# Ninety-two expert columns listed instead of 88, and three dense columns held back for the end of each PEER stage, in a two-layer decoder trunk on one core

## The chip, the core and the metric

The kernel runs on one core of a Trainium2 chip. A core has a matrix engine (PE), a vector engine (DVE), a scalar engine (ACT), GpSimd (POOL), a queue engine (SP) and 16 DMA engines. The metric is the device time of one execution in microseconds (us), as a median of several runs.

## The reference, cut to what matters

Two layers, 256 tokens of 1024 numbers, float32. Each layer is a token mixer, a layer norm, a PEER mixture of 16384 experts, a second layer norm and a gated addition:

```python
for i in range(DEPTH):                        # DEPTH = 2
    x = layer_norm(alpha * x + mix, ...)      # mix: SSD in layer 0, attention in layer 1
    ffn = peer_ffn(x, peer_w_q[i], peer_sub_keys[i], peer_u[i], peer_v[i])
    x = layer_norm(alpha * x + ffn, ln_ffn_g[i], ln_ffn_b[i])
    gate = jax.nn.sigmoid((x @ ple_w_gate[i]).astype(jnp.float32)).astype(x.dtype)
    x = x + gate * (p[i] @ ple_w_proj[i])

def block(xb):                                # in peer_ffn, 128 tokens at a time
    q = (xb @ w_q).reshape(PEER_TOKEN_BLOCK, PEER_HEADS, 2, PEER_HALF)
    ...                                       # 16 of 16384 experts for each token and head
    u_g = u[expert]
    v_g = v[expert]
    act = jax.nn.gelu(jnp.einsum('td,thkd->thk', xb, u_g).astype(f32))
    return jnp.einsum('thk,thkd->td', (gate * act).astype(v_g.dtype), v_g)
```

## The kernel before, in words

The experts of a layer are 128 columns of 128 experts. For every column the kernel computes the activations of all 256 tokens (`expert_in`, 16 matmuls against `u`) and multiplies them by the gates, which are zero for a token that did not pick the expert. Then the rows of `v` have to be summed with these weights. The 256 tokens are two blocks of 128; the sum lives in four PSUM banks, `accs[tb][h]`, block `tb` by half `h` of the 1024 outputs.

There are two ways to add a column. A **dense** column (`dense`, `expert_out`) loads 512 KB of `v` by the SP queue into a `raw` buffer, splits it on ACT (the high part, line 125) and DVE (the low part, line 126) into one of four `hl` buffers, splits its weights in the same way, and takes 12 matmuls of 512 columns: three products of high and low parts for each of the four banks (`mm3s`, line 151). The first `MANY` = 88 columns are **listed** instead. Their 88 x 128 experts are sorted into three classes by who picked them: both blocks, block 0 alone, block 1 alone; experts that nobody picked drop out. The picked ones are packed into groups of 128 (`CAPS`: 36 groups of `both`, 21 of `one`, 21 of `two`). A group fetches its 128 rows of `v`, and the 128 rows of weights that go with them, by two gathers on the POOL queue (line 1187), splits them like a dense column, and takes 12 matmuls if both blocks need it and 6 if one does. If a class has more experts than its groups hold, a loop behind a branch (`general`, `branch`) does all listed columns again for the surplus.

So that groups can fetch weights, the activations of the listed columns are written to DRAM (`keep`, 8 columns a call, ACT queue): block 0 twice, to a table for all groups (`w_d`) and to one for the `one` groups (`a_d`), and block 1 to `w_d`. The lists are made on DVE and PE in stages (`listing`, `stages`) that are laid under the last 12 `expert_in` steps and the first `LEAD` = 6 dense columns. `late(e)` finishes the activations of the last columns: it needs the sum of two halves that a POOL DMA `w<-w` (line 931) adds up in place, and then runs a GELU on ACT (line 950).

The order of the work is written out by hand. After the six leading dense columns come the 21 `one` groups mixed with `MIX` = 13 dense columns; then, in the part called **inner** here, the 36 `both` groups, 16 of the 21 `two` groups and the other 21 dense columns, spread evenly, with the loads of the gate weights (`w_pg`) among them; then the **tail**: the last `TAIL` = 5 `two` groups, which touch block 1 only. The last `both` group closes block 0, and the layer norm of block 0 (lines 205 to 226) runs on DVE, ACT and POOL while PE works on the five tail groups. The two transposes of the normed block (`turn`, line 191) stand on PE behind the fourth and the fifth of them (`TURNS`). Then come the gate matmuls (line 155).

An engine executes its instructions in the order in which they stand. Buffers come from pools: four `hl`, four `raw` of the SP queue, six `raw` and eight `rows_w` for gathers, five `w`.

Of the kernel before, what the change touches and what calls it, by code (L numbers as in the profile page):

```python
# [17 lines left out]
P = 128  # L18
T = 256
# [6 lines left out]
TAIL = 5  # L26
# [3 lines left out]
MANY = 88  # L30
# [5 lines left out]
CAPS = (36, 21, 21)  # L36
BASES = (0, 36, 57)
# [30 lines left out]
class Net:  # L68
# [688 lines left out]
    def peer(self, i):  # L757
        nc, dram = self.nc, self.dram
        with self.tc.tile_pool(name=f"peer{i}", bufs=1) as pool, ExitStack() as stack:
# [271 lines left out]
            def listing():  # L1031
# [73 lines left out]
                def place(j):  # L1105
                    if j == 0:
                        picked["list"] = self.aux()[:, :3 * MANY].rearrange("p (e k) -> p e k", k=3)
                    cs = slice(8 * j, 8 * j + 8)
                    o = ones[j % 2]
                    V.tensor_tensor(pairs(o), self.iota.rearrange("p (n j) -> p n j", j=2)[:, None].to_broadcast([P, 8, P // 2, 2]),  # L1110
                                    at_r[:, cs, None, :].to_broadcast([P, 8, P // 2, 2]), op=OP.is_equal)
                    for c in range(8):
                        nc.tensor.matmul(picked["list"][:, 8 * j + c], o[:, c], vals[:, 8 * j + c], start=True, stop=True)
# [36 lines left out]
                def ordered(k):  # L1150
                    with self.after((picked["turn"],) if k != 1 else ()):
# [4 lines left out]
                        *[lambda j=j: place(j) for j in range(MANY // 8)], keys, *[lambda k=k: ordered(k) for k in range(3)]]  # L1156
# [3 lines left out]
            def weights(e):  # L1160
                w = tl([P, 2, T], F32R, "w", 5)
                self.split(w[:, 0, :], w[:, 1, :], column(e))
                return w
# [4 lines left out]
            def expert_out(w, hl, start):  # L1168
                self.mm3s([(accs[tb][h], lambda a, tb=tb: w[:, a, tb * P:(tb + 1) * P],
                            lambda b, h=h: hl[:, b, h * 512:(h + 1) * 512]) for tb in range(2) for h in range(2)],  # L1170
                          start, lambda n: False)

            def fetched(s, hl=None):
                n = picked["n"] = picked["n"] + 1
                kind = sum(s >= b for b in BASES[1:])
                t = P if kind else T
                if kind == 1:
                    raw = early[n % 3][:, :1024] if n % 3 < 2 else self.raw()
                    some = early[n // 4 % 2][:, 1024 + P * (n % 4):1024 + P * (n % 4) + P]
# [11 lines left out]
                return kind, t, some, raw, hl  # L1191

            def group_load(s, hl=None):
                kind, t, some, raw, hl = fetched(s, hl)
                w = tl([P, 2, T], F32R, "w", 5)
                with self.after(picked["split"]):
                    self.split(w[:, 0, :t], w[:, 1, :t], some)
                    picked["split"] = self.split(hl[:, 0], hl[:, 1], raw)
                return kind, w, hl

            def group_out(kind, w, hl, ends=()):
                tbs = ((0, 1), (0,), (1,))[kind]
                self.mm3s([(accs[tb][h], lambda a, n=n: w[:, a, n * P:n * P + P],
                            lambda b, h=h: hl[:, b, h * 512:(h + 1) * 512]) for n, tb in enumerate(tbs) for h in range(2)],
                          False, lambda n: tbs[n // 2] in ends)

            def group(s):
                group_out(*group_load(s), (0,) if s == closing else ())

            def general():  # L1210
                raw, part, some = x[:, 0], pp[:, 0, :T], pp[:, 0, T:2 * T]
                hl, w = wide[0][:, 0], wide[0][:, 1, 0, :2 * T].rearrange("p (a t) -> p a t", a=2)
                with self.tc.For_i(0, MANY, 1) as c:
# [5 lines left out]
                    group_out(0, w, hl)  # L1219
# [8 lines left out]
            for hc in range(19):  # L1228
# [6 lines left out]
                if hc >= 7:  # L1235
# [13 lines left out]
            todo = [lambda c=c: keep(c, c + 8, 1) for c in range(0, MANY, 8)]  # L1249
# [38 lines left out]
            closing = [s for _, _, s in inner if s in both][-1]  # L1288
# [8 lines left out]
            wide = [new([P, 3, 2, 1024], "wide", F32R)]  # L1297
            pgw = {}

            def gate_load(n):  # L1300
                if n == 3:
                    wide.append(tl([P, 5, 2, 1024], F32R, "high"))
                hl = wide[0][:, n] if n < 3 else wide[1][:, n - 3]
# [15 lines left out]
            for k, (kind, w, hl) in enumerate(end):  # L1319
                group_out(kind, w, hl, (1,) if k == TAIL - 1 else ())  # L1320
# [135 lines left out]
```

## Time and profile before

| | |
|---|---|
| median of 3 runs | 1842.74 us (1841.68 to 1846.28) |
| the profiled execution | 1855.82 us, span 1854.0 us |
| PE busy | 1824.7 us, 98% of the span |
| weight loads of PE | 1554.5 us, 84% |
| DVE, ACT, POOL busy | 81%, 62%, 33% |
| mean DMA rate | 238 GB/s |
| mean granted PE clock | 0.995 of full speed |

The profiled execution is a single one and 13.1 us above the median. Times in the rows are microseconds from the start of its span. A busy PE is not a PE at its peak, since the ends of matmuls are modelled; how many matmuls finish in a stretch says more.

### The profile page before, as it was taken

The numbers are of one execution on the slowest core, as the hardware profiler recorded it, in microseconds if no ns is written. First come the engines' busy times: TensorE is split into PE (matmuls) and PEld (weight loads), VectorE is DVE, ScalarE is ACT, GpSimd is POOL, SyncE is SP. The second block draws the span as 40 slices with busy tenths as digits, with TensorE's granted clock in tenths as the row PEclk, the third lists the DMA queues.
The fourth block names the chain that finished last, engine by engine and source line by source line (L and its number), as shares of the span: only waits on it lengthen the run. The fifth ranks groups of instructions, "written<-read, shape, count | busy, mean of one in ns | idle before, by whom it ended". The sixth has DMA issues, their size and how long they took to land. (4 is left out here: it accounts for less than half of the span.)

```text
span 1854.0 us, 31864 instructions
## 1 busy us (share of the span) xinstructions
PE 1824.7 (98%) x11192; PEld 1554.5 (84%) x11192; DVE 1499.4 (81%) x2958; ACT 1157.6 (62%) x2322; POOL 604.0 (33%) x596
## 2 busy tenths in 40 slices
PE   8999999999999999999999999999999999989998
PEld 7998888888888888788877788888888887868887
DVE  7798789989989987676767778997998997657675
ACT  6865456697666656565646655669666665556563
POOL 0001003332222257766700001332222224776660
PEclk9999999999999999999999999999999999989999
DMA  7665669898799998989736566989779999888871
GB/s 263 204 192 177 218 181 228 218 238 203 183 273 331 270 314 277 333 271 321 268 100 199 182 205 189 225 218 244 195 185 283 320 282 284 284 291 283 313 241 55
DMA packets 211787, 442.13 MB, mean 238 GB/s; under 512 B 18756, under 2 KB 120296, under 8 KB 209960
## 3 DMA queue, kind: packets, MB, share of 16 engines
q1 hardware_dynamic: 77512, 275.14, 45.8%
q0 software_dynamic: 65472, 130.32, 27.3%
q10 hardware_dynamic: 68640, 34.61, 6.5%
q8 instruction: 89, 1.46, 0.3%
q14 instruction: 74, 0.61, 0.1%
HBM read 365.51 MB, written 40.93 MB: 219 GB/s over the span
## 5 line engine op out<-in xcount | busy, mean ns | idle before, releaser
L126 DVE TENSOR_TENSOR hl<-raw,hl 128x1024 fp32r<-128x1024 f32 x578 | 706.8, 1225 | 207.4 <-ACT hl L125 148.7
L167 PE MATMUL acc<-xT,hl 128*128 128x256 f32 (+1 forms) x4608 | 839.3, 339 | 2.0 <-DVE xT L194 0.8
L167 PEld LDWEIGHTS acc<-xT,hl 128*128 128x128 f32 x4608 | 700.7, 188 | 102.5 <-DVE hl L126 4.7
L125 ACT CAST hl<-raw 128x1024 fp32r<-128x1024 f32 x578 | 606.3, 1052 | 226.6 <-PE acc L151 108.4
L151 PE MATMUL acc<-hl,w 128*128 128x512 f32 x2316 | 538.4, 393 | 11.2 <-issue 3.6
L151 PEld LDWEIGHTS acc<-hl,w 128*128 128x128 f32 x2316 | 437.1, 190 | 110.5 <-issue 7.7
L931 POOL DMA_DIRECT2D w<-w x160 | 139.7, 873 | 392.9 <-ACT w L950 242.0
L931 POOL DMA_DIRECT2D act<-w x96 | 84.0, 875 | 303.8 <-ACT w L930 182.6
L1187 POOL DMA_INDIRECT raw<-in_v,r x128 | 141.3, 1104 | 94.8 <-DVE hl L126 35.4
L929 ACT COPY w<-acc 128x256 f32<-128x256 f32 x160 | 59.8, 374 | 165.3 <-PE acc L167 157.4
L1187 POOL DMA_INDIRECT rows_w<-w_d,r x114 | 132.1, 1159 | 34.7 <-issue 34.7
L155 PE MATMUL mm<-xT,hl 128*128 128x256 f32 x816 | 101.1, 284 | 2.1 <-ACT hl L125 1.0
L155 PEld LDWEIGHTS mm<-xT,hl 128*128 128x128 f32 x816 | 98.6, 192 | 3.7 <-ACT hl L125 1.5
L930 ACT COPY w<-acc 128x256 f32<-128x256 f32 x256 | 97.2, 380 | 0.0
L975 DVE TENSOR_TENSOR pick<-pick,r 128x2048 f16<-128x2048 f16 x64 | 78.2, 1222 | 0.9
L929 ACT COPY act<-acc 128x256 f32<-128x256 f32 x96 | 35.7, 372 | 69.1 <-PE acc L167 68.7
L991 PEld LDWEIGHTS <-pick 128*128 128x128 f16 x1024 | 66.4, 98 | 13.2 <-issue 11.1
L992 PE MATMUL mm<-pick 128*128 128x88 f16 x512 | 67.8, 203 | 0.0
L220 POOL TENSOR_TENSOR ln_s<-ln_s,mhalf 128x1 f32<-128x1 f32 x8 | 4.4, 552 | 179.2 <-PE acc L155 131.1
L542 POOL TENSOR_TENSOR sq<-sq,sqt 128x256 f32<-128x256 f32 x12 | 12.5, 1040 | 150.7 <-ACT sqt L541 150.4
L991 PE MATMUL aux<-pick 128*128 128x128 f16 x688 | 59.1, 220 | 0.5
L950 ACT ACTIVATE w<-w 128x256 f32<-128x256 f32 (+19 forms) x144 | 50.8, 353 | 8.7 <-DMA w<-w 8.7
(290 smaller groups left out, 2101.8 us busy)
## 6 DMA issues: line engine op xcount, KB each, us to landing
raw<-in_u SPq DMA_DIRECT2D x256, 512.0 KB
raw<-in_v SPq DMA_DIRECT2D x80, 512.0 KB
w_d<-act ACTq DMA_DIRECT2D x44, 512.0 KB
w<-w POOLq DMA_DIRECT2D x160, 128.0 KB
raw<-in_w_q SPq DMA_DIRECT2D x32, 512.0 KB
raw<-in_w_xbc SPq DMA_DIRECT2D x24, 512.0 KB
act<-w POOLq DMA_DIRECT2D x96, 128.0 KB
a_d<-act ACTq DMA_DIRECT2D x22, 512.0 KB
```

The costliest lines, as they stand in the source:

```text
L125: a = self.nc.scalar.copy(hi, src)
L126: b = self.nc.vector.tensor_tensor(lo, src, hi.bitcast(F32), op=OP.subtract)
L151: self.last_mm = self.nc.tensor.matmul(out, lhs(a), rhs(b), start=start and i == 0, stop=stop(n) and i == 2).ins
L155: self.last_mm = self.nc.tensor.matmul(out, lhs(a), rhs(b), start=start and i == 0, stop=stop and i == 2).ins
L167: self.nc.tensor.matmul(dst, hl[:, a, k * P:(k + 1) * P], src, start=k + a == 0, stop=(k, a) == order[-1] and k == KD - 1)
L929: nc.scalar.copy(whole, pe[:, :T])
L930: copied = nc.scalar.copy(pair[:, 1, :], pe[:, T:]).ins
L931: nc.gpsimd.dma_start(whole, pair[:, 1, :], accum_op=OP.add)
L975: nc.vector.tensor_tensor(a2, both, gates, op=OP.mult)
L991: nc.tensor.matmul(pg[:, t, :], one[:, 0, 4 * h + t], a2[:, 4 * h + t, k], start=k == 0, stop=k == 1)
L992: nc.tensor.matmul(banks["used"][:, MANY * tb:MANY * tb + MANY], one[:, 0, 4 * h + t], a2[:, 4 * h + t, 0, :MANY], start=at == 0, stop=at ...
L1187: got = nc.gpsimd.indirect_dma_start(out=dst, out_offset=None, in_=src, in_offset=rows(which))
```

## The change

The listed columns go from 88 to 92, and the groups from 36, 21 and 21 to 37, 22 and 22. The dense columns go from 40 to 36, and the last three of these (`LATER`) are not done in the inner part: their weights are split half-way through it, their `v` is loaded at its end, and their matmuls are cut in two. The halves for block 0 come first and close block 0. The halves for block 1 come behind, and then two `two` groups (`TAIL` = 2). The buffer `half` and a part of the tile `high` hold the high and low parts of the second of these groups, for which none of the four `hl` buffers is left. The list of 92 columns has one more step, of four columns.

```diff
-TAIL = 5
+TAIL = 2
+LATER = 3
-MANY = 88
+MANY = 92
-CAPS = (36, 21, 21)
-BASES = (0, 36, 57)
+CAPS = (37, 22, 22)
+BASES = (0, 37, 59)
...
             def keep_first():
-                c = kept[0]
-                if c + 8 <= min(now["ready"], MANY):
-                    keep(c, c + 8, 0)
-                    keep(c, c + 8, 0, first)
-                    kept[0] = c + 8
+                c, d = kept[0], min(kept[0] + 8, MANY)
+                if c < d <= now["ready"]:
+                    keep(c, d, 0)
+                    keep(c, d, 0, first)
+                    kept[0] = d
...
-            def expert_out(w, hl, start):
+            def expert_out(w, hl, start, tbs=(0, 1), ends=()):
                 self.mm3s([(accs[tb][h], lambda a, tb=tb: w[:, a, tb * P:(tb + 1) * P],
-                            lambda b, h=h: hl[:, b, h * 512:(h + 1) * 512]) for tb in range(2) for h in range(2)],
-                          start, lambda n: False)
+                            lambda b, h=h: hl[:, b, h * 512:(h + 1) * 512]) for tb in tbs for h in range(2)],
+                          start, lambda n: tbs[n // 2] in ends)
...
-            stages = [[classes], [*sums, ranks], [], [places, ones[0]], ones[1:3], ones[3:5], ones[5:7], ones[7:9], [*ones[9:11], surplus],
-                      [keys, one], [], [two], [both]]
+            stages = [[classes], [*sums, ranks], [], [places, ones[0]], ones[1:3], ones[3:5], ones[5:7], ones[7:9], ones[9:11],
+                      [ones[11], surplus], [keys, one], [], [two], [both]]
...
-            emit(inner, spread_over(dense, range(MANY + LEAD + MIX, P), 0.86), [(at, extra, f) for at, f in loads],
+            later = tl([P, LATER, 2, T], F32R, "pick", 2)
+            loads += [(0.5, lambda: [weights(P - LATER + k, later[:, k]) for k in range(LATER)])]
+            emit(inner, spread_over(dense, range(MANY + LEAD + MIX, P - LATER), 0.9), [(at, extra, f) for at, f in loads],
                  [(0.1, branch, None)])
-            end = []
-            for k, s in enumerate(last):
-                end.append(group_load(s, None if k else wide[1][:, 4]))
+            halves = [(later[:, k], self.chunk(dram["v"][i, P - LATER + k])) for k in range(LATER)]
+            end = [group_load(s, (half, wide[1][:, 8]) if k else None) for k, s in enumerate(last)]
+            for k, (w, hl) in enumerate(halves):
+                expert_out(w, hl, False, (0,), (0,) if k == LATER - 1 else ())
...
-            for k, (kind, w, hl) in enumerate(end):
-                group_out(kind, w, hl, (1,) if k == TAIL - 1 else ())
+            for k in range(LATER + TAIL):
+                if k < LATER:
+                    expert_out(*halves[k], False, (1,))
+                else:
+                    group_out(*end[k - LATER], (1,) if k == LATER + TAIL - 1 else ())
                 if k in TURNS[:2]:
                     self.turn(x, 0, TURNS.index(k))
```

Before, DVE at the end of layer 1: the splits of the last three tail groups (each a `w` and an `hl`) stand among the instructions of the norm of block 0, which begin with line 205.

```order
L126 TENSOR_TENSOR hl_19386<-raw_17921,hl_19386 128x1024
L126 TENSOR_TENSOR w_19395<-rows_w_17924,w_19395 128x128
L126 TENSOR_TENSOR hl_19394<-raw_17922,hl_19394 128x1024
L205 SCALAR_TENSOR_TENSOR last_17925,ln_s_19409<-last_17925,acc_17211 128x512
L126 TENSOR_TENSOR w_19403<-rows_w_17924,w_19403 128x128
L205 SCALAR_TENSOR_TENSOR last_17925,ln_s_19409<-last_17925,acc_17212 128x512
L126 TENSOR_TENSOR hl_19402<-raw_17923,hl_19402 128x1024
L207 TENSOR_SCALAR ln_s_19409<-ln_s_19409 128x1
L208 TENSOR_SCALAR ln_s_19409<-ln_s_19409 128x1
L218 SCALAR_TENSOR_TENSOR last_17928<-last_17925,ln_s_19409,last_17927 128x512 x2
```

The same place in the changed kernel, whose lines are numbered one higher here:

```order
L127 TENSOR_TENSOR hl_19311<-raw_19310,hl_19311 128x1024
L127 TENSOR_TENSOR hl_19316<-raw_19315,hl_19316 128x1024
L127 TENSOR_TENSOR hl_19321<-raw_19320,hl_19321 128x1024
L127 TENSOR_TENSOR hl_19327<-raw_17916,hl_19327 128x1024
L127 TENSOR_TENSOR w_19335<-rows_w_17921,w_19335 128x128
L127 TENSOR_TENSOR high_19151<-raw_17917,half_17927 128x1024
L206 SCALAR_TENSOR_TENSOR last_17922,ln_s_19359<-last_17922,acc_17183 128x512
L206 SCALAR_TENSOR_TENSOR last_17922,ln_s_19359<-last_17922,acc_17184 128x512
L208 TENSOR_SCALAR ln_s_19359<-ln_s_19359 128x1
L209 TENSOR_SCALAR ln_s_19359<-ln_s_19359 128x1
L219 SCALAR_TENSOR_TENSOR last_17925<-last_17922,ln_s_19359,last_17924 128x512 x2
```

The three dense splits (`raw_19310` to `raw_19320` come by the SP queue) and the two gathered ones (`raw_17916`, `raw_17917`) all stand ahead of the norm now, and nothing stands within it.

PE at that place in the changed kernel (`acc_17183` and `acc_17184` are block 0, `acc_17185` and `acc_17186` block 1, `pick_17928` the weights split early): the last matmuls of block 0, by the third held-back column, and the first of block 1, by the first.

```order
L152 MATMUL acc_17184<-hl_19321,pick_17928 128x512
L152 MATMUL acc_17183<-hl_19321,pick_17928 128x512
L152 MATMUL acc_17184<-hl_19321,pick_17928 128x512
L152 MATMUL acc_17185<-hl_19311,pick_17928 128x512
L152 MATMUL acc_17186<-hl_19311,pick_17928 128x512
```

Behind the close of block 0 stand 18 + 6 matmuls, then the first transpose, 6 matmuls and the second transpose; before, it was 24, the transpose, 6 and the transpose.

POOL where the lists are ready in layer 0, before: `w_7869`, `w_7910` and `w_7947` are the last three columns' sums, `pick<-a_d` and `pick<-in_v` the gathers of the first `one` groups (weights, then rows of `v`).

```order
L931 DMA w_7869<-w_7869 128x256
L1187 DMA pick_8104<-a_d_75,r_902_7452 128x128
L1187 DMA pick_8104<-in_v,r_902_7452 128x1024
L931 DMA w_7910<-w_7910 128x256
L1187 DMA pick_8104<-a_d_75,r_902_7452 128x128
L931 DMA w_7947<-w_7947 128x256
L1187 DMA pick_8105<-in_v,r_902_7452 128x1024
```

And in the changed kernel:

```order
L932 DMA w_7863<-w_7863 128x256
L932 DMA w_7904<-w_7904 128x256
L1189 DMA pick_8111<-a_d_75,r_902_7454 128x128
L1189 DMA pick_8111<-in_v,r_902_7454 128x1024
L932 DMA w_7954<-w_7954 128x256
L1189 DMA pick_8111<-a_d_75,r_902_7454 128x128
L1189 DMA pick_8112<-in_v,r_902_7454 128x1024
```

The sum of the last column but one (`w_7904`) now stands ahead of the first gather, and that of the last (`w_7954`) behind one pair of gathers instead of a pair and a half. Layer 1 has the same order.

## Rows read from the trace of the kernel before

**Rows 1.** The page's first part: busy microseconds of each engine, share of the span, instructions.

```profile
PE 1824.7 (98%) x11192; PEld 1554.5 (84%) x11192; DVE 1499.4 (81%) x2958; ACT 1157.6 (62%) x2322; POOL 604.0 (33%) x596
```

**Rows 2.** Busy time of each engine in four stretches of 50 us inside the two inner parts: the length, then busy us and (x instructions) of PE, PEld, DVE, ACT, POOL, then granted clock, DMA share and GB/s.

```profile
800.00:850.00 50.00, 50.00 (x222) 41.44 (x221) 34.74 (x46) 28.41 (x43) 33.17 (x32) 1.00 0.89 314
850.00:900.00 50.00, 50.00 (x223) 41.40 (x222) 31.74 (x42) 28.74 (x43) 30.86 (x28) 1.00 0.82 273
1700.00:1750.00 50.00, 50.00 (x222) 41.41 (x221) 33.76 (x45) 28.67 (x44) 32.22 (x29) 1.00 0.89 316
1750.00:1800.00 50.00, 50.00 (x222) 41.40 (x221) 35.10 (x45) 31.20 (x46) 30.80 (x28) 1.00 0.79 250
```

**Rows 3.** The timeline of PE at the end of layer 0 and of layer 1: start, us, engine, line, operation, tiles, count, and in brackets the idle time before and what ended it. The six matmuls into `acc` from `high` are the first tail group, the 18 the next three.

```profile
928.95 1.52 PE L151 MATMUL acc<-high,w 128*128 128x512 f32 x6
930.31 4.24 PE L151 MATMUL acc<-hl,w 128*128 128x512 f32 x18
936.70 0.66 PE L191 MATMUL mm<-ident,last 128*128 128x128 f32 x4 [2.14 <-DVE last L226]
937.11 1.64 PE L151 MATMUL acc<-hl,w 128*128 128x512 f32 x6
...
1816.21 4.24 PE L151 MATMUL acc<-hl,w 128*128 128x512 f32 x18
1822.35 0.74 PE L191 MATMUL mm<-ident,last 128*128 128x128 f32 x4 [1.90 <-DVE last L226]
1822.76 2.89 PE L151 MATMUL acc<-hl,w 128*128 128x512 f32 x6
```

**Rows 4.** The timeline of DVE at the end of layer 0: the norm of block 0 (from 930.65) with splits within it, and the norm of block 1 (from 938.96) with one instruction of a transpose within it.

```profile
930.65 0.68 DVE L205 SCALAR_TENSOR_TENSOR last<-last,acc 128x512 f32<-128x512 f32 x1
932.21 1.23 DVE L126 TENSOR_TENSOR hl<-raw,hl 128x1024 fp32r<-128x1024 f32 x1
933.35 0.21 DVE L207 TENSOR_SCALAR ln_s<-ln_s 128x1 f32<-128x1 f32 x1
935.89 1.42 DVE L226 SCALAR_TENSOR_TENSOR last<-last,ln_s,last 128x512 f32<-128x512 f32 x2 [0.69 <-POOL ln_s L220]
...
938.96 0.68 DVE L205 SCALAR_TENSOR_TENSOR last<-last,acc 128x512 f32<-128x512 f32 x1
940.17 0.69 DVE L194 TENSOR_TENSOR xT<-mm,xT 128x512 fp32r<-128x512 f32 x1
940.77 0.21 DVE L207 TENSOR_SCALAR ln_s<-ln_s 128x1 f32<-128x1 f32 x1
943.28 1.42 DVE L226 SCALAR_TENSOR_TENSOR last<-last,ln_s,last 128x512 f32<-128x512 f32 x2 [0.67 <-POOL ln_s L220]
```

**Rows 5.** The timeline of ACT at the end of layer 0: the high split of the last tail group.

```profile
931.13 1.05 ACT L125 CAST hl<-raw 128x1024 fp32r<-128x1024 f32 x1 [1.45 <-DMA raw<-in_v,r]
```

**Rows 6.** The timeline of ACT where the `one` groups begin, in layer 0 and in layer 1: `late` waits for the sum that POOL's DMA makes.

```profile
674.96 0.42 ACT L950 ACTIVATE w<-w 128x256 f32<-128x256 f32 x1 [3.46 <-DMA w<-w]
...
1552.45 0.42 ACT L950 ACTIVATE w<-w 128x256 f32<-128x256 f32 x1 [5.22 <-DMA w<-w]
```

**Rows 7.** The timeline of PE at the same two places, with the idle time that follows.

```profile
675.89 73.18 PE L151 MATMUL acc<-hl,w 128*128 128x512 f32 x318 [0.53 <-ACT w L950]
...
1553.39 68.87 PE L151 MATMUL acc<-hl,w 128*128 128x512 f32 x294 [2.29 <-ACT w L125]
```

**Rows 8.** The timeline of POOL at that place in layer 0.

```profile
665.04 1.08 POOL L1187 DMA_INDIRECT pick<-a_d,r  x1 [2.67 <-DVE r L1136]
666.42 1.00 POOL L1187 DMA_INDIRECT pick<-in_v,r  x1 [0.30 <-DVE w L126]
667.42 1.03 POOL L931 DMA_DIRECT2D w<-w  x1
```

**Rows 9.** Groups of the whole trace (count, busy us, mean ns of one, idle before): the matmuls that count who picked which listed column, and the comparison on DVE for one step of the list; then the timeline's row of one such step on PE.

```profile
L992 PE MATMUL mm<-pick 128*128 128x88 f16 x512 | 67.8, 203 | 0.0
L1110 DVE TENSOR_TENSOR pick<-iota,pick 128x1024 f16<-128x1024 f16 x22 | 14.5, 688 | 0.7 <-PE aux L1113 0.6
...
643.86 0.35 PE L1113 MATMUL aux<-pick 128*128 128x3 f16 x8
```

**Rows 10.** Groups of POOL's instructions from 739 to 791 us, at the start of layer 0's inner part: count, busy us, mean ns of one, idle before.

```profile
L1187 POOL DMA_INDIRECT rows_w<-w_d,r x19 | 22.6, 1191 | 5.8 <-issue 5.8
L1187 POOL DMA_INDIRECT raw<-in_v,r x18 | 19.1, 1064 | 5.5 <-issue 5.2 <-DMA raw<-in_v,r 0.3
```

**Rows 11.** The timeline of POOL in that stretch, its first and its last fetch of weights; 18 groups were fetched from the one to the other.

```profile
739.03 1.58 POOL L1187 DMA_INDIRECT rows_w<-w_d,r  x1 [0.30 <-issue]
...
790.83 0.95 POOL L1187 DMA_INDIRECT rows_w<-w_d,r  x1 [0.30 <-issue]
```

**Rows 12.** What POOL waited for from 772 to 926 us: us in total, times, the longest.

```profile
POOL raw L1187 <- DVE hl L126: 18.3, 11, 4.7
POOL raw L1187 <- DVE w L126: 11.1, 7, 2.8
```

**Rows 13.** The columns of rows 2 for the start of the inner part, in layer 0, in layer 1, and for 10 us within the latter.

```profile
740.00:800.00 60.00, 57.70 (x253) 46.82 (x252) 39.02 (x53) 34.33 (x53) 43.67 (x40) 1.00 0.89 309
1610.00:1660.00 50.00, 45.08 (x174) 34.07 (x173) 26.87 (x39) 22.84 (x36) 36.13 (x31) 0.90 0.83 286
1640.00:1650.00 10.00, 7.50 (x31) 5.32 (x30) 3.12 (x4) 1.78 (x4) 7.87 (x8) 0.94 0.91 332
```

More of the change, by code (lines that the diff above doesn't have):

```diff
@@ L1107, in place @@
                         picked["list"] = self.aux()[:, :3 * MANY].rearrange("p (e k) -> p e k", k=3)
[L1108 to L1112, printed above, removed]
+                    n = min(8, MANY - 8 * j)
+                    cs = slice(8 * j, 8 * j + n)
+                    o = ones[j % 2][:, :n]
+                    V.tensor_tensor(pairs(o), self.iota.rearrange("p (n j) -> p n j", j=2)[:, None].to_broadcast([P, n, P // 2, 2]),
+                                    at_r[:, cs, None, :].to_broadcast([P, n, P // 2, 2]), op=OP.is_equal)
+                    for c in range(n):
                         nc.tensor.matmul(picked["list"][:, 8 * j + c], o[:, c], vals[:, 8 * j + c], start=True, stop=True)
@@ L1155, in listing, with weights @@
                 return [classes, lambda: sums(0, 4), lambda: sums(4, 7), ranks, places, surplus,
-                        *[lambda j=j: place(j) for j in range(MANY // 8)], keys, *[lambda k=k: ordered(k) for k in range(3)]]
+                        *[lambda j=j: place(j) for j in range(-(-MANY // 8))], keys, *[lambda k=k: ordered(k) for k in range(3)]]
             accs = []
-            def weights(e):
-                w = tl([P, 2, T], F32R, "w", 5)
+            def weights(e, w=None):
+                w = tl([P, 2, T], F32R, "w", 5) if w is None else w
                 self.split(w[:, 0, :], w[:, 1, :], column(e))
@@ L1197, in group_load @@
                     self.split(w[:, 0, :t], w[:, 1, :t], some)
-                    picked["split"] = self.split(hl[:, 0], hl[:, 1], raw)
+                    picked["split"] = self.split(*hl, raw)
                 return kind, w, hl
@@ L1203, in group_out @@
                 self.mm3s([(accs[tb][h], lambda a, n=n: w[:, a, n * P:n * P + P],
-                            lambda b, h=h: hl[:, b, h * 512:(h + 1) * 512]) for n, tb in enumerate(tbs) for h in range(2)],
+                            lambda b, h=h: hl[b][:, h * 512:(h + 1) * 512]) for n, tb in enumerate(tbs) for h in range(2)],
                           False, lambda n: tbs[n // 2] in ends)
             def group(s):
-                group_out(*group_load(s), (0,) if s == closing else ())
+                group_out(*group_load(s))
             def general():
@@ L1218, in general @@
                     self.split(hl[:, 0], hl[:, 1], raw)
[L1219 removed]
+                    group_out(0, w, (hl[:, 0], hl[:, 1]))
             def branch(_):
@@ L1245, in peer @@
             *ones, keys, both, one, two = steps[6:]
-            stages = [[classes], [*sums, ranks], [], [places, ones[0]], ones[1:3], ones[3:5], ones[5:7], ones[7:9], [*ones[9:11], surplus],
-                      [keys, one], [], [two], [both]]
+            stages = [[classes], [*sums, ranks], [], [places, ones[0]], ones[1:3], ones[3:5], ones[5:7], ones[7:9], ones[9:11],
+                      [ones[11], surplus], [keys, one], [], [two], [both]]
             assert kept[0] == MANY
-            todo = [lambda c=c: keep(c, c + 8, 1) for c in range(0, MANY, 8)]
+            todo = [lambda c=c: keep(c, min(c + 8, MANY), 1) for c in range(0, MANY, 8)]
             lates = [lambda e=e: late(e) for e in range(P - 3, P)]
@@ L1296, in peer @@
             x, pp, gb0, gb1 = (new([P, 2, D], f"last{k}") for k in range(4))
-            wide = [new([P, 3, 2, 1024], "wide", F32R)]
+            wide, half = [new([P, 3, 2, 1024], "wide", F32R)], new([P, 1024], "half", F32R)
             pgw = {}
@@ L1301, in gate_load @@
                 if n == 3:
-                    wide.append(tl([P, 5, 2, 1024], F32R, "high"))
-                hl = wide[0][:, n] if n < 3 else wide[1][:, n - 3]
+                    wide.append(tl([P, 9, 1024], F32R, "high"))
+                hl = wide[0][:, n] if n < 3 else wide[1][:, 2 * n - 6:2 * n - 4]
                 raw = (gb0, gb1)[n // 2][:, n % 2] if n < 3 else None
```

3 lines of the change are left out of this document (1 added, 2 removed).

## The prediction

> **What bounds the kernel now.** I read four views, in this order. The page's first part says that PE is busy for 98% of the span [rows 1]. That alone proves little, so I counted matmuls in stretches of the inner part [rows 2]. In four stretches of 50 us, two in each layer, PE finishes 222 or 223 matmuls of 512 columns with no idle time: 50.00 / 222 = 0.2252 us each. It is the same number whether the DMA engines are 0.79 or 0.89 busy and move 250 or 316 GB/s. So there PE sets the pace, and a matmul less is 0.2252 us less. Then I looked for the places where PE does not run at this rate. There are three in a layer. Where the `one` groups begin, PE stands still for 0.53 us in layer 0 and 2.29 us in layer 1 [rows 7], while ACT waits 3.46 and 5.22 us for a sum that a POOL DMA makes [rows 6]. At the start of the inner part PE finishes 253 matmuls in 60 us, where 60 / 0.2252 = 266 fit, and 174 in 50 us in layer 1, where 222 fit [rows 13]; POOL issues gathers without a longer pause than 0.3 us in that stretch [rows 10]. And at the tail PE waits 2.14 and 1.90 us for the norm of block 0 [rows 3].
>
> The profiled execution took 1855.8 us, 13.1 us over the median of 1842.7. The loss at the start of layer 1's inner part, (222 - 174) x 0.2252 = 10.8 us with a granted clock of 0.90 [rows 13], is most of that, and layer 0 shows that it need not be so large. I make the sum in the profiled execution's terms, leave that loss out of the gains, and apply the sum to the median.
>
> **The change part by part.**
>
> *Matmuls.* Before, a layer sums its experts in 36 x 12 + 42 x 6 + 40 x 12 = 1164 matmuls; now in 37 x 12 + 44 x 6 + 36 x 12 = 1140. A held-back column still takes 12, in two halves. 24 fewer in two layers, at 0.2252 us [rows 2]: **-10.8 us**. The groups must hold the experts, or the surplus loop runs. Counting the picks of the reference on its inputs, 92 columns need 36.2 and 36.3 groups of `both`, 21.0 and 20.8 of `one`, 20.7 and 21.1 of `two`. They fit into 37, 22 and 22.
>
> *The norm of block 0.* Behind its close stand 24 matmuls ahead of the first transpose, before and after: 24 x 0.2252 = 5.4 us of cover. In layer 0 the tail starts at 928.95, its 24 matmuls end at about 934.5, and the transpose starts at 936.70 [rows 3]. The norm takes that long because DVE works in order: its first instruction starts 1.7 us after the close, at 930.65, and a split of 1.23 us stands in its middle, at 932.21 [rows 4]. This split waits for ACT, and ACT for the last gather, until 931.13 [rows 5]. The norm of block 1 shows the chain without that: from 938.96 to the end of the first half of line 226, 943.28 + 0.71 = 943.99, so 5.03 us, of which 0.60 (940.17 to 940.77) belong to a transpose [rows 4]. That leaves 4.4 us, less than the 5.4 of cover. In the changed order all five splits stand ahead of the norm, and 18 block-0 matmuls (4.05 us) cover them. The wait goes: **-4.0 us** (2.14 + 1.90). The bound below is 0, if the last gather lands more than 1 us after the close. In layer 1 the six matmuls behind the wait took 2.89 us instead of 1.64 [rows 3]; those 1.25 us I leave out and keep for the range.
>
> *Where the `one` groups begin.* ACT's wait is for a sum that POOL issued at 667.42, right behind a gather of 512 KB at 666.42 [rows 8], and that was complete by 674.96 [rows 6]. Now the sum of the last column but one goes ahead of the first gather, and that of the last behind one pair. PE lost 0.53 + 2.29 = 2.82 us there [rows 7]. One of the two sums still stands behind a gather, so I take half: **-1.4 us**, between 0 and -2.8. DVE gets half a step of the list more in the same stretch, 0.688 / 2 = 0.34 us [rows 9]; the `expert_in` matmuls beside it hide that, and uncovered it would cost those 0.34 us in each layer.
>
> *The longer list.* 512 counting matmuls get 4 more columns. By the rate of rows 2 a column costs 0.2252 / 512 us, so 512 x 4 of them cost 0.9 us; as the row's 203 ns are longer than its 88 columns take at that rate [rows 9], 0 is possible. Four list matmuls more a layer, at 0.35 / 8 us [rows 9], are 0.35 us in two layers. **+1.2 us**, between 0.3 and 1.3. Three more `keep` DMAs a layer are issued by ACT; their bytes grow by 4 in 88, and they end long before the groups that read them.
>
> *Gathers.* A layer fetches 81 groups instead of 78, and SP loads four dense columns fewer, so DVE and ACT split 117 instead of 118 and the bytes stay about the same. But the supply moves from SP to POOL. Before, the inner part has 36 x 12 + 16 x 6 + 21 x 12 = 780 matmuls (175.7 us) and 52 groups: one every 3.38 us. Now it has 37 x 12 + 20 x 6 + 14 x 12 = 732 matmuls (164.8 us) and 57 groups: one every 2.89 us. POOL without pause fetched 18 groups from 739.03 to 790.83 [rows 11], one every 2.88 us. Before, it gained half a microsecond a group, filled its buffers, and then waited for DVE to free them, 18.3 + 11.1 us in 154 [rows 12]. Now it just keeps up, and the shortage at the start of the inner part is not made good. That shortage cost (266 - 253) x 0.2252 = 3 us in layer 0 [rows 13]. More of the same is bounded by 0, if the lead with which POOL enters suffices, and by 10.8 us a layer, which is layer 1's. I take 2 us a layer, near layer 0's: **+4 us**, between 0 and +22. At the end there is no new danger: before, five `two` groups came in a row at 1.35 us of matmuls each; now there are two, behind 36 matmuls of the held-back columns.
>
> Sum: -10.8 - 4.0 - 1.4 + 1.2 + 4 = **-11.0 us**. In the profiled terms that is 1844.8 us, and from the median **1831.7 us**.
>
> What speaks against it: in 10 us of the stalled stretch, with DVE busy for 3.12 us, POOL issued 8 gathers, four groups, one every 2.5 us [rows 13]; with DVE busier its instructions took 1191 and 1064 ns on average [rows 10] and one group every 2.88. So gathers seem slower beside DVE. [...]
>
> **Rivals.**
>
> *Supply by bytes.* If the stretches with a DMA share near 0.9 were bound by DMA, the unchanged bytes would take the unchanged time, and only the tail's 4.0 and the 1.4 would be gained, less 1.2: -4.2 us, **1838.5 us**. For it: the DMA shares of 0.79 to 0.89. Against: the equal matmul counts [rows 2]. [...]
>
> *POOL becomes the bound (slower).* 57 groups a layer at a pace p cost 57 x (p - 2.89) more once p is over 2.89. In two layers each 0.1 us is 11.4 us. The gain is gone at p = 2.89 + 11.0 / 114 = 2.99. At 3.1 the sum is -11 + 24 = +13, **1856 us**. For it: the pace of 2.88 is at the edge. Against: 2.5 in the stalled stretch, so a starved DVE lets POOL go faster, which damps it.
>
> *The cover fails again.* If the last gather still lands late, DVE holds the norm and the 4.0 us stay: **1835.7 us**. Before, it landed at 931.13 with POOL behind; now only two groups follow the inner part.
>
> **How the numbers follow.** No change is what lies within 0.3%, 5.5 us, since the runs of this kernel spread by 4.6 us. I give the forecast 0.54, the failing cover 0.14, the bound by bytes 0.19, a POOL bound 0.13. Faster by over 5.5 us (below 1837.2): most of the first two, 0.66. Same: the bytes and small POOL losses, 0.23. Slower: 0.11. The low end takes all bounds that gain: -10.8 - 4.0 - 1.25 - 2.8 + 0.3 = -18.6, so 1824; the high end reaches into the POOL case, 1846 (p = 3.02). By itself the likeliest case spans 1824 to 1837.
>
> **What would show it.** In the profile after: 48 fewer matmuls of 512 columns at the same 222 in 50 us (right), or fewer in 50 us (bytes or POOL); no wait of PE for line 227 ahead of the first transpose; DVE's first norm instruction within 0.7 us of the close; ACT's wait for `w<-w` shorter; POOL without its 29 us of waits for DVE in the inner part, and PE's count in its first 60 us not far below 253. Wrong: PE waits for splits spread over the inner part, or a granted clock below 1.00 there.

## The result, and the profile after

The changed kernel takes 1826.85 us (median of 7 runs, 1824.28 to 1834.61) against 1842.74 for the kernel before beside it: a ratio of 0.9921 with a 95% interval of 0.9895 to 0.9947, so 14.6 us less (9.8 to 19.3); the two medians by themselves are 15.9 us apart. Measured once more, it was 0.9913 (0.9890 to 0.9936), 16.0 us less. The forecast was 1831.7 us, 11.0 less, between 1824 and 1846. Its profiled execution took 1825.7 us, its span is 1823.9. Line numbers are one or two higher than before: the matmul is line 152, the high split on ACT 126, the low split on DVE 127, the transpose 192, the gathers 1189.

The page's first part, which answers to [rows 1]: there are 40 instructions less on PE (48 summing matmuls gone, eight for the list added), and 18.6 us less of its busy time.

```profile
PE 1806.1 (99%) x11152; PEld 1543.8 (85%) x11152; DVE 1493.5 (82%) x2948; ACT 1155.7 (63%) x2326; POOL 629.4 (35%) x608
```

Stretches of the inner part, with the columns of [rows 2, 13]; the layer 1 stretch at 1660 us is that layer's worst:

```profile
740.00:800.00 60.00, 59.31 (x259) 48.18 (x258) 41.30 (x55) 36.70 (x55) 47.81 (x41) 1.00 0.88 308
800.00:850.00 50.00, 50.00 (x222) 41.39 (x222) 33.97 (x47) 30.66 (x49) 39.32 (x36) 1.00 0.92 334
...
1660.00:1700.00 40.00, 38.09 (x161) 30.98 (x160) 25.59 (x37) 22.51 (x37) 31.47 (x29) 0.96 0.88 306
1700.00:1750.00 50.00, 50.00 (x222) 41.40 (x221) 34.09 (x46) 28.64 (x44) 39.64 (x35) 1.00 0.87 296
```

The pace of 222 matmuls in 50 us is unchanged. Away from it the inner part loses 266 - 259 = 7 matmuls in layer 0 and 178 - 161 = 17 in layer 1, together 24 x 0.2252 = 5.4 us. In layer 1 about half of this is a stop of 1.91 us (40.00 - 38.09), and the rest goes with the granted clock of 0.96. Behind that stands the supply. POOL's waits from 757 to 917 us, the answer to [rows 12] (total, times, longest), and then ACT's waits for PE and for gathered rows over the whole run, in the kernel before (lines 125 and 151) and in the changed one:

```profile
POOL rows_w L1189 <- issue: 14.6, 48, 0.3
POOL raw L1189 <- issue: 13.1, 43, 0.3
POOL raw L1189 <- DVE hl L127: 1.2, 4, 0.3
...
ACT hl L125 <- PE acc L151: 120.5, 84, 5.9
ACT hl L125 <- DMA raw<-in_v,r: 24.4, 13, 3.8
...
ACT hl L126 <- DMA raw<-in_v,r: 105.3, 65, 5.8
ACT hl L126 <- PE acc L152: 52.2, 43, 3.2
```

POOL no longer waits for DVE beyond its own step of 0.3 us between instructions. It runs without a pause, and ACT, which had waited mostly for PE, now waits mostly for the rows that POOL fetches, 105 us in a run.

The tail of layer 0 on PE and, behind the dots, on DVE, where [rows 3, 4] showed waits:

```profile
916.13 8.32 PE L152 MATMUL acc<-hl,pick 128*128 128x512 f32 x36
924.29 1.52 PE L152 MATMUL acc<-hl,w 128*128 128x512 f32 x6
925.65 0.66 PE L192 MATMUL mm<-ident,last 128*128 128x128 f32 x4
...
919.28 1.22 DVE L127 TENSOR_TENSOR high<-raw,half 128x1024 fp32r<-128x1024 f32 x1
920.42 0.68 DVE L206 SCALAR_TENSOR_TENSOR last<-last,acc 128x512 f32<-128x512 f32 x1
```

Block 0 closes 18 matmuls after 916.13, at about 920.2. The last split ends at 920.5, the norm starts 0.2 us after the close and has no split within, and the transpose follows its matmuls with no wait.

### The profile page after: what moved, and what is told of

Same layout as the page of the kernel before. It is cut to its first block, busy times and chain, and to the rows that moved or that the text cites. A ratio compares the mean times of both kernels' runs of the same rounds, so it can differ in the third digit from the quotient of the medians.

```text
span 1823.9 us, 31779 instructions
## 1 busy us (share of the span) xinstructions
PE 1806.1 (99%) x11152; PEld 1543.8 (85%) x11152; DVE 1493.5 (82%) x2948; ACT 1155.7 (63%) x2326; POOL 629.4 (35%) x608
## 4 chain that ended last, share of the span: by engine, by line
PE 46%; DVE 4%; issue 3%; POOL 2%; ACT 2%; DMA 1%; POOLq 0%; DVEq 0%; ACTq 0%
PE acc L152 18%; PE acc L168 17%; PE acc L156 5%; PE mm L168 2%; POOL raw L1189 1%; DVE hl L127 1%; PE aux L992 1%; DMA raw<-in_v,r 1%; POOL rows_w L1189 1%; ACT hl L126 1%; PE mm L993 1%; PE mm L992 1%; PE aux L800 0%; DMA raw<-in_u 0%; DVE high L836 0%
## 5 line engine op out<-in xcount | busy, mean ns | idle before, releaser
L127 DVE TENSOR_TENSOR hl<-raw,hl 128x1024 fp32r<-128x1024 f32 x574 | 699.3, 1221 | 197.0 <-ACT hl L126 190.5
L152 PE MATMUL acc<-hl,w 128*128 128x512 f32 x2196 | 502.2, 390 | 3.5 <-ACT hl L126 2.4
L152 PEld LDWEIGHTS acc<-hl,w 128*128 128x128 f32 x2196 | 412.5, 188 | 92.4 <-ACT hl L126 3.8
L1189 POOL DMA_INDIRECT raw<-in_v,r x132 | 153.4, 1162 | 40.2 <-issue 32.6
L1189 POOL DMA_INDIRECT rows_w<-w_d,r x118 | 141.7, 1201 | 36.0 <-issue 32.0
L930 ACT COPY act<-acc 128x256 f32<-128x256 f32 x96 | 35.7, 372 | 68.5 <-PE acc L168 68.1
L993 PE MATMUL mm<-pick 128*128 128x92 f16 x512 | 68.1, 204 | 0.0
L1189 POOL DMA_INDIRECT pick<-a_d,r x44 | 52.2, 1187 | 14.9 <-issue 11.6
```

What stands on the lines that cost most here:

```text
L127: b = self.nc.vector.tensor_tensor(lo, src, hi.bitcast(F32), op=OP.subtract)
L152: self.last_mm = self.nc.tensor.matmul(out, lhs(a), rhs(b), start=start and i == 0, stop=stop(n) and i == 2).ins
L930: nc.scalar.copy(whole, pe[:, :T])
L993: nc.tensor.matmul(banks["used"][:, MANY * tb:MANY * tb + MANY], one[:, 0, 4 * h + t], a2[:, 4 * h + t, 0, :MANY], start=at == 0, stop=at ...
```

## The experiments

The experiments stand in three sets, each on a chip of its own, with the kernel before beside them: its median was 1841.65 us in the first set, 1857.72 in the second and 1843.78 in the third. Kernels are compared within a set. A difference in microseconds is the ratio's distance from 1, times that median.

**The tail alone (first set).** 88 columns and the old list steps, but the new tail.

```diff
-MANY = 92
+MANY = 88
...
-CAPS = (37, 22, 22)
-BASES = (0, 37, 59)
+CAPS = (36, 21, 21)
+BASES = (0, 36, 57)
...
-            stages = [..., ones[7:9], ones[9:11],
-                      [ones[11], surplus], [keys, one], [], [two], [both]]
+            stages = [..., ones[7:9], [*ones[9:11], surplus],
+                      [keys, one], [], [two], [both]]
```

> The tail alone: 88 columns and 36, 21 and 21 groups as before, but three dense columns are held back and two `two` groups end the stage. Matmuls and gathers keep their number (1164 matmuls and 78 groups a layer); the inner part has 762 matmuls and 55 groups, one every 3.12 us, so POOL at 2.88 us keeps up. My theory (the 4.0 us that PE waited for the norm of block 0 go, nothing else changes): 4 us less than before, between 2.8 and 6, no wait of PE for line 227 ahead of the first transpose, first norm instruction within 0.7 us of the close. The rival that the wait was covered by other work anyway: 0, with the idle time turning up in the gate matmuls behind. If the whole 14.6 us of the change came from the tail, it would be 14.6 us here.

Measured: 0.9983 (0.9966 to 1.0001), 3.1 us less (6.3 less to 0.2 more). PE in layer 0, and ACT's wait for the sum (total, times, longest):

```profile
923.50 8.32 PE L152 MATMUL acc<-hl,pick 128*128 128x512 f32 x36
931.66 1.52 PE L152 MATMUL acc<-hl,w 128*128 128x512 f32 x6
933.02 0.65 PE L192 MATMUL mm<-ident,last 128*128 128x128 f32 x4
...
ACT w L951 <- DMA w<-w: 8.0, 2, 4.5
```

The wait for the norm is gone, the wait where the `one` groups begin is still there. The time fits the 4 us and does not exclude zero.

**The list alone (first set).** 92 columns, the new list steps, the old tail.

```diff
-TAIL = 2
-LATER = 3
+TAIL = 5
...
-            emit(inner, spread_over(dense, range(MANY + LEAD + MIX, P - LATER), 0.9), ...
+            emit(inner, spread_over(dense, range(MANY + LEAD + MIX, P), 0.86), ...
...
-            for k in range(LATER + TAIL):
-                if k < LATER:
-                    expert_out(*halves[k], False, (1,))
-                else:
-                    group_out(*end[k - LATER], (1,) if k == LATER + TAIL - 1 else ())
+            for k in range(TAIL):
+                group_out(*end[k], (1,) if k == TAIL - 1 else ())
```

> The list alone: 92 columns, 37, 22 and 22 groups and the later list as in the changed kernel, but the tail of before (five `two` groups behind the close, no columns held back). My theory (PE's pace): 48 matmuls less at 0.2252 us are 10.8, the earlier sums give up to 2.8, the longer list costs 1.2; the inner part has 750 matmuls and 54 groups, one every 3.13 us, so gathers cost nothing here: 10 to 12.4 us less than before, and PE still waits about 2 us a layer ahead of the first transpose. The rival by bytes: 0 to 2 us less. The rival that POOL binds: over 1850.

Measured: 0.9935 (0.9911 to 0.9959), 12.0 us less (7.6 to 16.4). PE's wait for the norm over the run, and its longest stretch without a stop in layer 0:

```profile
PE mm L191 <- DVE last L226: 2.8, 2, 1.6
...
768.46 151.22 PE L151 MATMUL acc<-hl,w 128*128 128x512 f32 x666 [0.15 <-PEq L1225]
```

So most of the gain comes with the list alone, and PE goes through its matmuls with no stop between, 151.22 / 666 = 0.2271 us each. The kernel moves 443.2 MB where the kernel before moved 442.1, so the rival by bytes (0 to 2 us) falls. The list alone also carries the later list steps; the next kernel has these without the 48 matmuls.

**The list steps alone (first set).** The kernel before, with its list one step later.

```diff
-..., ones[7:9], [*ones[9:11], surplus], [keys, one], [], [two], [both]]
+..., ones[7:9], ones[9:11], [surplus], [keys, one], [], [two], [both]]
```

> The kernel before with its list steps set one step later, as the changed kernel has them (keys and the `one` order in the step of the last but one `expert_in`), nothing else. My theory: the sum of the last but one column goes ahead of the first gather on POOL, ACT's waits of 3.46 and 5.22 us for `w<-w` shrink to under 1 us, and PE's 2.82 us of idle time where the `one` groups begin go at least by half: 1.4 to 2.8 us less, and up to 5 if the clock's loss there goes with it. The rival that one step later only moves the wait to the first gathers: 0, with an ACT wait for `pick` in place of that for `w<-w`.

Measured: 0.9991 (0.9973 to 1.0010), 1.7 us less (5.0 less to 1.8 more): zero lies within the interval, so the time shows no gain, but it leaves most of the 12.0 us to the matmuls. The trace speaks more clearly: ACT in layer 0, where [rows 6] has 3.46 us, PE where [rows 7] has 0.53 us, and PE through layer 0's inner part.

```profile
672.02 0.42 ACT L950 ACTIVATE w<-w 128x256 f32<-128x256 f32 x1 [1.02 <-DMA w<-w]
...
669.59 14.79 PE L151 MATMUL acc<-hl,w 128*128 128x512 f32 x64 [0.21 <-DVE w L126]
...
734.76 188.92 PE L151 MATMUL acc<-hl,w 128*128 128x512 f32 x831
```

The last row is a surprise: here the inner part of the kernel before runs through with no stop, where [rows 13] has 13 matmuls too few. I come back to it.

**96 columns (first set).** The changed kernel, carried on.

```diff
-MANY = 92
+MANY = 96
...
-CAPS = (37, 22, 22)
+CAPS = (38, 22, 23)
```

> The changed kernel carried on to 96 columns: 38, 22 and 23 groups, 1110 matmuls a layer instead of 1140, 83 groups instead of 81. The inner part has 702 matmuls (158.1 us) and 59 groups, one every 2.68 us, less than the 2.88 us that POOL took. If PE still sets the pace: 60 x 0.2252 = 13.5 us less than the changed kernel, about 1813. If POOL sets it at 2.88 us a group: 59 x 0.20 = 11.8 us a layer more, so about 10 us more than the changed kernel, 1837. If a starved DVE lets POOL go at 2.5 to 2.7 us a group: between, 1813 to 1826. My estimate 1828, with PE waiting for splits all over the inner part and ACT for gathers.

Measured: 0.9944 (0.9926 to 0.9962), median 1830.58 us. The changed kernel itself was not timed on this chip; the list alone beside it took 1825.34, 5.2 us less with as many matmuls as the changed kernel, and all but one of its six runs lie below this median. The changed kernel's two ratios from elsewhere, 0.9921 and 0.9913, would be 4 to 6 us less, with intervals that overlap. So 60 matmuls fewer, worth 13.5 us, brought no gain. PE's wait for splits over the run, ACT's for gathers, and POOL's first and last fetch of weights in the inner part and tail of layer 0:

```profile
PE acc L152 <- ACT hl L126: 11.6, 8, 2.7
...
ACT hl L126 <- DMA raw<-in_v,r: 127.3, 75, 5.3
...
741.21 1.05 POOL L1189 DMA_INDIRECT rows_w<-w_d,r  x1 [0.30 <-issue]
...
915.35 1.84 POOL L1189 DMA_INDIRECT rows_w<-w_d,r  x1 [0.30 <-issue]
```

61 groups were fetched, so the pace is (915.35 - 741.21) / 60 = 2.90 us where 2.68 would be needed. POOL sets the pace, and the rival of the prediction in which it does comes true four columns further on.

**One more instruction on POOL (second set).**

```diff
                     picked["order"] = (got.ins,)
+                if kind != 1:
+                    nc.gpsimd.memset(spare, 0.0)
```

> The changed kernel with one more small instruction on POOL (a memset of 128x1 that nobody reads) behind the two gathers of each `both` and `two` group, 59 a layer, 57 of them in the inner part. The dose per group is what the trace shows for it; POOL's smallest instruction so far, on 128x1, took 0.55 us, so 0.1 to 0.55 us. If POOL is at its limit (pace 2.88 us against a demand of 2.89): each 0.1 us costs up to 2 x 57 x 0.1 = 11.4 us, less what starved gathers gain; for 0.3 us 15 to 34 us more than the changed kernel. If POOL has room (the bound is PE alone): 0 to 2 us more, with ACT's waits for gathers unchanged.

**The large loads in pieces (second set).**

```diff
-            loads = [(0.65, lambda: nc.sync.dma_start(x, self.x_d[i])), (0.7, lambda: nc.sync.dma_start(pp, self.pp_d[i])),
+            loads = [(0.6 + 0.04 * k + at, lambda dst=dst, src=src, b=k % 2, c=slice(512 * (k // 2), 512 * (k // 2) + 512):
+                      nc.sync.dma_start(dst[:, b, c], src[i][:, b, c]))
+                     for at, dst, src in ((0.0, x, self.x_d), (0.02, pp, self.pp_d)) for k in range(4)]
```

> The changed kernel with the loads of `x` and `pp`, 1 MB each on the SP queue in the inner part, cut into four pieces of 256 KB each and spread from 0.60 to 0.74 of the inner part. In layer 1 of the changed kernel ACT waited 5.75 and 4.39 us for gathered rows just while the two loads were under way, and PE finished 161 matmuls where 178 fit (3.8 us). If the large loads hold up the gathers: these waits fall under 3 us and the time by 2 to 4 us. If it is POOL's pace that leaves no lead: the same waits at some other place, and 0 within 1.5 us.

**No branch (second set).**

```diff
-emit(..., [(0.1, branch, None)])
+emit(...)
```

> The changed kernel without the branch and the surplus loop behind it (left out; with these inputs the loop has no work). My prediction laid the loss at the start of layer 1's inner part (174 matmuls where 222 fit, 10.8 us) to a shortage of gathers; in that trace the last stop of PE ends at the branch. If the branch is what costs there in some runs: 1 to 3 us less than the changed kernel in the median, and a narrower spread than 1824 to 1835. If gathers: the same time within 1 us and the same spread.

**Two columns held back (second set).**

```diff
-TAIL = 2
-LATER = 3
+TAIL = 3
+LATER = 2
```

> The changed kernel with two columns held back instead of three and three `two` groups at the end instead of two. The inner part has 738 matmuls and 56 groups: one group every 2.97 us instead of 2.89, further from POOL's 2.88. The halves ahead of the close are 12 matmuls (2.7 us) instead of 18 (4.05), and behind the close 24 stand ahead of the first transpose as before. If the loss that is left in the changed kernel (259 matmuls of 266, 161 of 178: 5.4 us in two layers) is POOL's pace: 2 to 5 us less. If the shorter cover lets the splits run into the norm again: up to 1.3 us of PE's wait in each layer, so 0 to 2.6 us more. My estimate: 2 us less than the changed kernel.

Measured on this chip: 1.0035 (1.0000 to 1.0071) with the extra instruction, 0.9988 (0.9956 to 1.0019) with the pieces, 0.9978 (0.9951 to 1.0005) without the branch, 0.9958 (0.9926 to 0.9991) with two held back. What the traces show first is something else. PE's waits (total, times, longest) in these four, in this order, and the extra instruction's group (count, busy, mean ns):

```profile
PE acc L152 <- PEq L1228: 14.6, 2, 14.5
PE acc L152 <- issue: 9.1, 11, 2.4
...
PE acc L152 <- PEq L1226: 10.2, 1, 10.2
PE acc L152 <- issue: 8.1, 10, 2.1
...
PE acc L152 <- issue: 13.8, 16, 4.9
...
PE acc L152 <- issue: 6.8, 17, 1.3
...
L1192 POOL MEMSET spare<- 128x1 f32 x118 | 11.6, 98 | 21.1 <-DMA pp_d<-pr 14.4
```

PE stops in the inner part for "issue" (nothing that the profile shows) or at the branch ("PEq"), 7 to 24 us in a run. None of the nine traces of the changed kernel and its variants outside this set has more than 0.2 us of this. The profiled execution of the kernel before has it too, 4.7 us in a run, most of it just where [rows 13] shows the loss in layer 1:

```profile
1647.37 0.96 PE L151 MATMUL acc<-hl,w 128*128 128x512 f32 x3 [1.60 <-issue]
...
1655.26 159.76 PE L151 MATMUL acc<-hl,w 128*128 128x512 f32 x696 [1.09 <-PEq L1224]
```

Taking the branch away does not take the stops away, and the runs spread as widely as before (1846.5 to 1865.9 us). POOL goes on fetching during such a stop and gets ahead, so these four say little on the supply. The dose of 0.098 us a group came with 7 and 12 us more in the median than the pieces and the kernel without the branch, which fetch as many groups; that is near the 2 x 57 x 0.1 = 11.4 of a POOL at its limit, but the changed kernel itself was not timed on this chip, and I leave all four open.

**The changed kernel, the list alone, fewer gathers and 94 columns, side by side (third set).** The second is the list alone again. The third skips the weights' gather of most `two` groups, so that their share of the sum is left out; the fourth is the list alone with two columns more.

```diff
-for dst, src, which in pairs:
+for dst, src, which in pairs[1 if kind == 2 and n > 32 else 0:]:
...
-MANY = 92
+MANY = 94
...
-CAPS = (37, 22, 22)
+CAPS = (38, 22, 22)
```

> The changed kernel itself, as the yardstick for the three kernels beside it on the same chip. 0.992 of the kernel before, within 0.0895 to 0.0947 above 0.9 as first measured (0.9895 to 0.9947), and a trace in which POOL fetches group after group without a wait in the inner part.

> The list alone once more (92 columns, tail of before), now beside the changed kernel on one chip. It differs from it by the held-back columns alone: 54 groups with 750 matmuls in the inner part instead of 57 with 732. If the tail adds its full gain to that of the list: 4 us more than the changed kernel. If the held-back columns pay for it with gathers that come too late in the inner part (5.4 us lost there in the changed kernel's trace): the same time within 2 us, with PE's wait of 1 to 2 us a layer for the norm, and no wait of PE for a split in the inner part.

> The changed kernel with POOL relieved: the `two` groups from the eleventh group of the inner part on do not fetch their weights and use those that lie in their buffer (that part of the sum is left out). Some 18 of 59 groups a layer save 1.2 + 0.3 us of POOL, 27 us in 165. All splits and matmuls stay. If POOL's pace still costs time in the changed kernel: ACT waits for gathers 30 to 60 us less over the run, and the time is 2 to 5 us less, most of what PE loses there (161 matmuls of 178 in 1660 to 1700 us). If PE alone is the bound: the same within 1.5 us.

> 94 columns with the tail of before: 38, 22 and 22 groups, 1128 matmuls a layer, no columns held back. The inner part has 738 matmuls and 55 groups, one every 3.02 us, so POOL at 2.88 us keeps up. By PE's pace: 24 x 0.2252 = 5.4 us less than the list alone at 92 columns, and 1 to 5 us less than the changed kernel. If the supply is already the bound at one group every 3.0 us: no less than the list alone at 92 columns.

| | median us | ratio to before (95%) |
|---|---|---|
| changed kernel | 1827.97 | 0.9913 (0.9890 to 0.9936) |
| list alone, 92 columns | 1827.25 | 0.9908 (0.9883 to 0.9933) |
| changed, fewer gathers | 1823.44 | 0.9889 (0.9865 to 0.9912) |
| list alone, 94 columns | 1826.38 | 0.9899 (0.9875 to 0.9923) |

PE's waits of the first, the second (two rows), the third and the fourth, then ACT's wait for gathers in the first, the second and the third, and POOL's waits for DVE from 757 to 917 us in the trace of the list alone on the first chip:

```profile
PE acc L152 <- ACT hl L126: 6.8, 4, 3.3
...
PE mm L191 <- DVE last L226: 2.4, 2, 1.5
PE acc L151 <- ACT hl L125: 1.4, 3, 0.6
...
PE acc L152 <- ACT hl L126: 1.5, 1, 1.5
...
PE mm L191 <- DVE last L226: 5.8, 2, 3.7
...
ACT hl L126 <- DMA raw<-in_v,r: 93.5, 57, 4.4
...
ACT hl L125 <- DMA raw<-in_v,r: 34.8, 24, 3.3
...
ACT hl L126 <- DMA raw<-in_v,r: 46.2, 24, 4.0
...
POOL raw L1188 <- DVE w L126: 7.7, 6, 2.2
POOL raw L1188 <- DVE hl L126: 6.2, 8, 1.9
```

With the list in place, the held-back columns bring nothing that can be measured: the list alone is 0.7 us below the changed kernel in the median, where the full gain of the tail would have put it 4 us above. The 2.4 us of waiting for the norm go, and more waits for splits come: 6.8 us here and 2.4 in the first trace of the changed kernel, against 1.4 here and none in the first trace of the list alone. Without the held-back columns POOL still has 13.9 us to wait for DVE in layer 0, with them it has none. Relieving POOL of 36 of 118 gathers of weights takes 4.5 us off the median, and five of its six runs lie below the lowest of the changed kernel; so the supply costs about that. The run does not say whether it is POOL's time or the traffic: it also moves 2.4 of 443 MB less. 94 columns save 24 matmuls (5.4 us), but the last gathers come later and the norm waits 5.8 us: 1.6 us below the changed kernel in the median, with intervals that overlap. No kernel here that computes the whole sum is shown to beat the changed one.

## Why the prediction was right, point by point

**Matmuls, -10.8.** Right. The pace of 0.2252 us held, and the list alone gave 12.0 and 17.0 us less, intervals 7.6 to 16.4 and 12.4 to 21.6, against the 10 to 12.4 expected. The list alone carries the later list steps too, but these by themselves gave 1.7 us, with zero in the interval. The rival of the bytes is out: matmuls fewer, bytes no fewer, time less. The Trainium skill ("Perfetto Trace Analysis", § Identifying the Most-Contended Engine) holds the busy share of matmuls to be no good measure of how close PE is to its limit. This case agrees: the share was 98% before and 99% after, and it was the count of matmuls in a stretch that told what one less is worth.

**The norm of block 0, -4.0.** Right as a mechanism: the wait is 0 in the changed kernel's tail, and the tail alone gave 3.1 us less (0 not excluded). But it was not an independent term, and beside the list its 4.0 us did not show in the time. Held-back columns take matmuls out of the inner part and leave their gathers in, so they tighten the supply from one group every 3.13 us (list alone) to one every 2.89. The prediction had this demand in its gather term, but did not set the tail's gain against the part of that term which the tail itself causes: the two about cancel. That the sum still came out near is in part because it held both.

**Where the `one` groups begin, -1.4.** Undersized. ACT has no wait for `w<-w` left, and PE's stops fell from 2.82 to 0.40 + 0.37 us:

```profile
670.51 13.69 PE L152 MATMUL acc<-hl,w 128*128 128x512 f32 x59 [0.40 <-DVE w L127]
...
1535.97 9.36 PE L152 MATMUL acc<-hl,w 128*128 128x512 f32 x40 [0.37 <-DVE w L127]
```

I had taken half, since one sum still stands behind a pair of gathers. It does, but ACT now comes to it later, at 676.44 in layer 0, and finds it done. A second part I had not priced at all: the clock. Before, 20 us around the stop in layer 1, and after, 30 us there:

```profile
1540.00:1560.00 20.00, 17.23 (x69) 13.10 (x68) 15.93 (x51) 10.69 (x22) 10.56 (x11) 0.91 1.03 324
...
1530.00:1560.00 30.00, 29.63 (x134) 24.23 (x133) 25.55 (x69) 19.45 (x35) 21.70 (x19) 1.00 1.01 333
```

Before, 69 matmuls where 89 fit are 4.5 us, of which 20.00 - 17.23 = 2.8 are stops, so some 1.7 us are lost at a granted clock of 0.91. It need not be so in every execution: the tail alone, whose list steps are those of before, has stops of 1.1 us in these 20 us at a granted clock of 1.00, and 81 matmuls:

```profile
1540.00:1560.00 20.00, 18.91 (x81) 14.66 (x81) 16.75 (x44) 12.20 (x22) 12.68 (x11) 1.00 0.96 305
```

With the 1.7 us of the one execution, with 2.05 instead of 1.4 us for the stops, and with the 1.25 us of the tail that I had left out, the sum becomes -11.0 - 0.65 - 1.7 - 1.25 = -14.6; with the list and the gathers at the sizes below, +0.65 and +5.4, it is -13.8. Measured were -14.6 and -16.0. These sizes were read afterwards from single executions, so the closeness is a fit and no test.

**The longer list, +1.2.** It was 0.3 us for the counting matmuls, 68.1 instead of 67.8, near the lower bound: four columns more hardly lengthen them. With the 0.35 us of list matmuls that is 0.65.

```profile
L993 PE MATMUL mm<-pick 128*128 128x92 f16 x512 | 68.1, 204 | 0.0
```

**Gathers, +4.** The size was about right, half of its reason wrong, and so in part luck. Right: POOL came to its limit, its 29 us of waits for DVE went, and what PE lost is 5.4 us by the counts and 4.5 us by the run with fewer gathers. Wrong: I read the losses of [rows 13] as a shortage of gathers, and took the 2 us a layer from them. The row of the list steps alone (831 matmuls in 188.92 us) shows that the inner part of the kernel before need have no such shortage, and in its own trace 4.7 of the 6.7 us of stops that belong to these losses end on "issue" and at the branch. I had counted matmuls there without reading what PE's brackets name.

**The rivals.** POOL as the bound was the close one: at 96 columns 13.5 us of matmuls are saved and the time is no less. Its price, 57 x (p - 2.89) a layer, came out too high. The pace of 2.88 was read from 52 us; over its 59 fetches in layer 0 of the changed kernel POOL took (911.47 - 738.35) / 58 = 2.98 us a group (first and last rows below). By the formula that costs 2 x 57 x 0.09 = 10.3 us and nearly the whole gain; the counts show 5.4. The formula takes no account of the lead with which POOL enters the inner part, but no run measured what that lead is worth. The faster pace of 2.5 us, seen where DVE stood still [rows 13], did not come to the rescue at 96 columns: it stayed at 2.90.

```profile
738.35 1.04 POOL L1189 DMA_INDIRECT rows_w<-w_d,r  x1 [0.30 <-issue]
...
911.47 1.04 POOL L1189 DMA_INDIRECT rows_w<-w_d,r  x1 [0.30 <-issue]
```

## What to carry to other kernels

Work that is moved between engines changes the demand per unit of the other engine, so set the slowest supplier's pace against the demand for each part of the change alone and for all together: two edits that would each gain can draw on one reserve. A bound that comes near shows in who waits: here ACT's waits turned from PE to gathers while PE still counted 222 in 50 us, and four columns more then saved nothing. Before a loss is put down to a shortage, read what ended the stop.

## What the runs showed of the hardware

The same program, the kernel before, took 1841.65, 1857.72 and 1843.78 us on three chips. On the slowest, PE, ACT and DVE stop together in the inner part, at the branch or for nothing that the profile shows, and of the changed kernel's four variants three gained only 0.1 to 0.4% and one nothing. That this is the chip's doing is not shown: each set ran on one chip only, and the first profile of the kernel before has such stops as well. ACT at such a place in the kernel with the extra POOL instruction, while POOL went on fetching (the bracket says "remote" and names no engine):

```profile
773.71 1.04 ACT L126 CAST hl<-raw 128x1024 fp32r<-128x1024 f32 x1 [4.93 <-remote]
...
785.11 1.04 ACT L126 CAST hl<-raw 128x1024 fp32r<-128x1024 f32 x1 [10.05 <-remote]
```

The matmuls pay for it a second time: in the stretch from 750 to 800 us of that kernel the granted clock is 0.83, and 134 matmuls finish where 222 fit. The 88 that are missing are 19.8 us, of which 50.00 - 33.10 = 16.9 are stops.

```profile
750.00:800.00 50.00, 33.10 (x134) 26.25 (x133) 22.31 (x31) 20.66 (x33) 31.58 (x29) 0.83 0.74 254
```

The traces give the stops no cause. The run without the branch shows that the branch alone is not it; no other run looked for one, and it stays open.
